# A finished head's accumulator is copied out of its bank by DVE ahead of two exps, in place of ACT between them

## The chip, the cores and the metric

The kernel runs on one core of one Trainium2 chip. The metric is the device time of one execution in microseconds. Before the change three runs took 3089.30, 3089.61 and 3089.72 us: a median of 3089.61 us. One further execution was profiled. It took 3089.38 us, of which 3087.6 us lie between its first and its last instruction (the span).

Names of engines: PE or TensorE (matmuls; PEld are its weight loads), DVE or VectorE, ACT or ScalarE, POOL or GpSimd, SP (issues DMAs). Each works through its own instructions strictly in the order in which the program has issued them.

## The reference

One layer of an encoder over 4096 tokens with 16 meta tokens ahead of them. What matters here is the attention branch: 8 query heads over 2 key/value heads, each of dimension 64, softmax over all 4112 keys, no mask.

```python
def gqa_block(q_blk, k, v):
    s = jnp.einsum('bkgqd,bksd->bkgqs', q_blk, k).astype(jnp.float32) * (HEAD_DIM ** -0.5)
    p = jax.nn.softmax(s, axis=-1)
    return jnp.einsum('bkgqs,bksd->bkgqd', p.astype(v.dtype), v)
...
a_out = attention_branch(q, k, v, q_norm_g[i], k_norm_g[i], cos, sin, n_tok) * jax.nn.silu(a_gate)
mixed = jnp.concatenate([f_out, a_out], axis=-1)
h = h + jnp.einsum('ble,ed->bld', mixed, w_out[i])
```

Beside it runs a Fourier branch (a DFT over positions and channels), then an output projection with residual, and a final RMSNorm.

## The kernel before

`phase_a` makes the projections (until some 770 us), `phase_b` the DFT, the attention and the output. All of what follows is in `phase_b`. The order of the work on each engine is the order of the calls in the program (`tc.manual_schedule()`); the framework adds only the semaphores that the data need.

**Tiling.** Queries go in 8 blocks b of 512. For each block there are 4 pairs p of heads, so the main loop (L1449) runs over 32 pairs i. A pair has two heads, one after the other, and each head 33 units: one for each chunk of 128 keys, in the order `SEQ` (the meta chunk first, then 0, 1, 4, 5, 2, 3, 6, 7, 8, 9, 12, ...). Unit j of a pair has number n = j % 33 within its head. `step` makes the four parts of a unit:

- `qk` (L1195): scores of 128 keys x 512 queries in a PSUM bank `s`. There are two such banks (`pq`). A chunk with n % 8 < 4 starts a bank anew (two matmuls, L1202 and L1203). The chunk four further on is kept as a difference of keys and is added on top of that bank (one matmul, L1198, and a half matmul in `low`, L1207), after the first chunk's exp has read it. So each score matmul waits for the exp of an earlier unit.
- `low` (L1205): the half matmuls of two difference chunks, run together.
- `ex` (L1209): ACT computes exp into `pe` (L1212); then DVE or POOL subtracts the upper 16 bits, giving the rest `rr` in 16 bits (L1214).
- `pvm` (L1217): nine matmuls (L1229 to L1236) that add the unit's probabilities times V, in high and low parts, to the head's accumulator `o`, a bank of the pool `pv` with one buffer. The next head's first `pvm` must therefore wait until the last head's `o` has been read. For the last unit, `pvm` returns `end`.

**The end of a head.** `end` (L1240) copies 452 columns of `o` to `tt` (L1243, ACT), takes the reciprocal of the sums (L1245, DVE), and four POOL instructions (L1247 to L1250) add the parts, multiply by the gate and by the reciprocal, and put the result in `ob`.

**Order of a unit.** In the loop over j: `qk()`, then a matmul of the output projection of the block before (`plan`, L1309; in units with n % 4 != 0). At the units with n = 4, 8, ..., 32 (`RUNS`) the `low` of two units follows; then `draw()` issues four matmuls of the row-maximum work of the next pair (`grp` in `max_units`, L1119); then `ex` of the two units; then one of two `parts` of the row-maximum work (a relu on ACT, L1124, and a max pass on DVE, L1125). The other units with n % 4 != 3 have their `ex` and one part. At the end of each unit its `pvm` is put in `pend`, and the one of five units before is issued (`LAG` = 5). At n = 4 the last `pvm` of the old head is drawn ahead of `low` (L1478), and its `end` is issued between the two `ex` (L1486). At the very end of the loop the last head's `end` comes from `flush`.

**Who subtracts.** `on_dve` (L1458): units with n = 0 and with n % 4 of 2 or 3 on DVE, the others on POOL; in the last pair DVE has every j not divisible by 3.

**The first five pairs** (`block0`) run the DFT's matmuls and the work behind them between the units, in place of the output projection. The last pair has no row-maximum work. After the loop a tail does the output projection of the last block.

In the text "the first run" of a head is the stretch from its units 3 and 4's `low` (n = 4) to the next `low` (n = 8); "the second run" is from n = 8 to n = 12.

Of the kernel before, what the change touches and what calls it, by code (L numbers as in the profile page):

```python
# [26 lines left out]
AF = mybir.ActivationFunctionType  # L27
# [768 lines left out]
def phase_b(tc, a, pool, mm3, id32, id16, sc):  # L796
# [5 lines left out]
    V, S, T, G = nc.vector, nc.scalar, nc.tensor, nc.gpsimd  # L802
# [4 lines left out]
    with ExitStack() as st:  # L807
# [383 lines left out]
        def step(h, kv, t, n, qa, qb, acc, banks, ob, gate, last):  # L1191
            d = {}
            cs = slice(n * P, (n + 1) * P)

            def qk():  # L1195
                if n < NT and n % 8 >= 4:
                    s = d["s"] = banks.pop(n - 4)
                    T.matmul(s, K[kv][:, 0, cs], qa, start=False, stop=False, skip_group_check=True)  # L1198
                else:
                    late = kv and last and n < NT and n // 2 % 2  # L1200
                    s = d["s"] = banks[n] = (pm if late else pq).tile([P, 512], F32, tag="m" if late else "s", name="s")
                    T.matmul(s, K[kv][:, 0, cs], qa, start=True, stop=False)  # L1202
                    T.matmul(s, K[kv][:, 1, cs], qb, start=False, stop=True)  # L1203

            def low(x):  # L1205
                r = slice(64 * x, 64 * x + 64)
                T.matmul(d["s"], K[kv][r, 1, cs], (qb if x else qa)[r], start=False, stop=True, skip_group_check=True)  # L1207

            def ex(eng):  # L1209
                pe = wk.tile([P, 512], F32, tag="pe", name="pe")  # L1210
                rr = wk.tile([P, 512], F16, tag="rr", name="rr")
                S.activation(pe, d["s"], AF.Exp, scale=HD ** -0.5)  # L1212
                hi = pe.bitcast(BF16)[:, 1::2]
                eng.tensor_tensor(out=rr, in0=pe, in1=hi, op=ALU.subtract)  # L1214
                d["hi"], d["rr"] = hi, rr

            def pvm():  # L1217


                if t == 0:  # L1220
                    acc.append(pv.tile([P, 512], F32, tag="o", name="o"))
                o = acc[0]
                hi, rr = d["hi"], d["rr"]
                vh, va, vl = VV[:, n, kv, :65], VV[:, n, kv], VV[:, n, kv, 65:129]
                for s in range(4):
                    cs = slice(s * P, (s + 1) * P)
                    c0 = s * 129
                    if s < 3:
                        T.matmul(o[:, c0:c0 + 129], hi[:, cs], va, start=t == 0 and s == 0, stop=t == NT,  # L1229
                                 skip_group_check=True)  # L1230
                    else:
                        T.matmul(o[:, c0:c0 + 65], hi[:, cs], vh, start=False, stop=t == NT,  # L1232
                                 skip_group_check=True)
                        T.matmul(o[:, c0:c0 + 64], hi[:, cs], vl, start=False, stop=t == NT,  # L1234
                                 skip_group_check=True)
                    T.matmul(o[:, c0:c0 + 65], rr[:, cs], vh, start=False, stop=t == NT, skip_group_check=True)  # L1236
                if t < NT:
                    return

                def end():  # L1240
                    tt = w2.tile([P, 452], F32, tag="tt", name="tt")
                    rc = sm.tile([P, 4], F32, tag="rc", name="rc")
                    S.activation(tt, o[:, :452], AF.Copy)  # L1243
                    tv = tt[:, :387].rearrange("p (s c)->p s c", s=3)
                    V.reciprocal(out=rc, in_=tt[:, 64:452:129])  # L1245
                    dst = ob[:, :, h * HD:(h + 1) * HD]
                    G.tensor_tensor(out=dst[:, 0:3], in0=tv[:, :, 0:64], in1=tv[:, :, 65:129], op=ALU.add)  # L1247
                    G.tensor_tensor(out=dst[:, 0:3], in0=dst[:, 0:3], in1=gate[:, 0:3], op=ALU.mult)
                    G.tensor_tensor(out=dst[:, 3], in0=tt[:, 387:451], in1=gate[:, 3], op=ALU.mult)
                    G.tensor_tensor(out=dst, in0=dst, in1=rc.unsqueeze(2).broadcast_to([P, 4, HD]), op=ALU.mult)  # L1250

                return end

            return qk, low, ex, pvm
# [187 lines left out]
        def flush():  # L1442

            end = pend.pop(0)()
            if end:
                end()

        prev = None
        for i, (b, p) in enumerate(pairs):  # L1449
            if p == 1 and b + 1 < NQB:  # L1450
                qload(b + 1)
            if i > 4:
                load_xr(b - 1, p)
            elif i == 4:
                load_mf(0, 0)
            ready = {}
            halves = out_units(b - 1, p) if b > 0 else None
            on_dve = {j for j in range(66) if j % 33 == 0 or j % 33 % 4 in (2, 3)}  # L1458
            if i + 1 == len(pairs):
                on_dve = {j for j in range(2 * NT + 2) if j % 3}  # L1460
            units = stream(i)
            plan = {}
            if halves:
                plan = dict(zip(OUT if i > 4 else OUT0, halves[0][0] + halves[0][1]))
            for j, (qk, half, ex, pvm) in enumerate(units):
                n = j % 33
                if n == 5:
                    for z in (j, j + 1):
                        if z in plan:
                            plan.pop(z)()  # L1470
                qk()
                if j == 63 and i + 1 < len(pairs):
                    fin_()
                    put_()
                if j in plan:
                    plan[j]()
                if j in RUNS:
                    end = pend.pop(0)() if n == 4 and pend else None  # L1478
                    units[j - 1][1](0)
                    half(1)  # L1480
                    more = draw()
                    if more:
                        parts.extend(more())
                    for x in (j - 1, j):
                        units[x][2](V if x in on_dve else G)
                        if end:  # L1486
                            end()
                            end = None
                    if parts:
                        parts.pop(0)()  # L1490
                elif n % 4 != 3:
                    ex(V if j in on_dve else G)
                    if parts:
                        parts.pop(0)()
                if j == (TR if i > 4 else 12) and b > 0:
                    low = out_tr(b - 1, p)
                last = {}
                if i + 1 < len(pairs):
                    meta_, red_, fin_, put_ = ends.get(i + 1, (None,) * 4)
                    last = {60: red_}  # L1500
                    if j == MT and meta_:
                        meta_[0]()
                if j in last:
                    last[j]()
                if i < 5:
                    block0(66 * i + j, j - 2 in RUNS)
                if i == 4 and j == 28:
                    load_xr(0, 0)
                if i == 4 and j == 6:
                    ready = dict(zip((7, 8, 9), mf_parts(0, 0)))  # L1510
                if i + 1 == len(pairs):
                    if 20 <= j < 60 and j % 11 == 9:
                        load_mf(b, j // 11 - 1)
                    if j >= 26 and j % 11 == 4:
                        ready = dict(zip((j, j + 1, j + 2), mf_parts(b, j // 11 - 2)))
                elif i >= 4:
                    if j == 40:
                        load_mf(*divmod(i - 3, 4))
                    if j == 47:
                        ready = dict(zip((48, 52, 53), mf_parts(*divmod(i - 3, 4))))  # L1520
                if j in ready:
                    ready[j]()
                if j == LAG + 2 and i + 1 < len(pairs):
                    gload(i + 1)
                if j == 20 and i + 1 == len(pairs):
                    load_xr(b, 0)
                if j == (TR if i > 4 else 12) + 1 and b > 0:
                    low()
                if j in NORM and prev:
                    prev[NORM.index(j)]()  # L1530
                if j == 65 and b > 0:
                    prev = out_end(b - 1, p, halves[1])
                pend.append(pvm)
                if len(pend) > LAG:
                    flush()
# [222 lines left out]
```

## Time and profile before

| | |
|---|---|
| median of three runs | 3089.61 us |
| the profiled execution | 3089.38 us, span 3087.6 us |
| granted TensorE clock, mean | 0.997 |
| PE / PEld busy | 3033.3 / 1798.9 us |
| DVE / ACT / POOL busy | 2248.5 / 2013.2 / 1737.6 us |
| L1243, the copy on ACT | 64 times, 542 ns each, 34.7 us |
| L1212, exp on ACT | 2112 times, 611 ns each |
| L1125, max pass on DVE | 1024 times, 689 ns each |

A row of the timeline reads: start in us from the span's start, duration in us, engine, line, operation, output <- inputs, shapes, number of like instructions merged in the row, and in brackets how long the engine had been idle before it and what ended that. Ends of matmuls are modelled, their starts are not. A row of a line's own view has the count, the shortest, median and longest duration in ns, and the first and the last start in us.

### The profile page before, as it was taken

How to read it: one execution, taken by the hardware profiler on the slowest of the kernel's cores; microseconds unless marked ns; L12 is line 12 of the kernel's file. 1: busy time of each engine (PE TensorE's matmuls, PEld its weight loads, DVE VectorE, ACT ScalarE, POOL GpSimd, SP SyncE). 2: the span in 40 equal slices, each digit the busy share in tenths (PEclk: the TensorE clock that was granted, in tenths of full speed). 3: DMA queues.
4: the chain of work that ended last, by engine and by line, in shares of the span. 5: the costliest groups of instructions: out<-in, count | busy, mean ns of one | idle time of the engine just before them, and what ended most of it. 6: DMA issues, size and time to landing. Idle time of an engine off the chain costs nothing.

```text
span 3087.6 us, 80210 instructions
## 1 busy us (share of the span) xinstructions
PE 3033.3 (98%) x32000; PEld 1798.9 (58%) x32000; DVE 2248.5 (73%) x4865; ACT 2013.2 (65%) x3936; POOL 1737.6 (56%) x1642
## 2 busy tenths in 40 slices
PE   8999999998999999999999999999999999999998
PEld 4555555555666655555555555555555555555564
DVE  6656565656878777777777777777777777777775
ACT  6434333325777777777777777777777777777763
POOL 4655555644767655555555555555555555555552
PEclk9999999999999999999999999999999999999999
DMA  7545445555521221112112111211121121111112
GB/s 243 183 149 172 133 139 169 166 179 181 135 74 43 79 55 29 33 35 49 29 32 43 43 33 32 50 29 39 29 50 29 39 46 33 32 32 29 39 41 71
DMA packets 236765, 235.23 MB, mean 76 GB/s; under 512 B 136949, under 2 KB 180949, under 8 KB 233573
## 3 DMA queue, kind: packets, MB, share of 16 engines
q1 hardware_dynamic: 222564, 204.93, 23.6%
q10 hardware_dynamic: 13824, 25.17, 2.2%
q8 instruction: 250, 4.10, 0.5%
q14 instruction: 127, 1.03, 0.1%
HBM read 131.14 MB, written 66.38 MB: 64 GB/s over the span
## 4 chain that ended last, share of the span: by engine, by line
PE 70%; ACT 2%; DVE 1%; POOL 1%; issue 1%; ACTq 0%; POOLq 0%; DVEq 0%
PE o L1229 12%; PE po L1309 10%; PE o L1236 8%; PE s L1198 7%; PE s L1202 7%; PE s L1203 7%; PE m L1119 6%; PE s L1207 5%; PE o L1234 2%; PE o L1232 2%; PE m L1557 1%; ACT pe L1212 1%; POOL rr L1214 1%; PE pd L913 1%; DVE rl L1125 0%
## 5 line engine op out<-in xcount | busy, mean ns | idle before, releaser
L1212 ACT ACTIVATE pe<-s 128x512 f32<-128x512 f32 x2112 | 1242.4, 611 | 571.9 <-PE s L1207 516.7
L1214 POOL TENSOR_TENSOR rr<-pe 128x512 f16<-128x512 f32 x1014 | 1131.3, 1133 | 797.4 <-ACT pe L1212 797.2
L1214 DVE TENSOR_TENSOR rr<-pe 128x512 f16<-128x512 f32 x1098 | 890.0, 812 | 275.3 <-ACT pe L1212 272.2
L1236 PE MATMUL o<-VV,rr 128*128 128x65 f16 x8448 | 974.7, 193 | 1.9 <-POOL rr L1214 1.8
L1236 PEld LDWEIGHTS <-rr 128*128 128x128 f16 x8448 | 784.2, 98 | 186.2 <-POOL rr L1214 3.1
L1125 DVE CUSTOM_DVE_ANT_0 rl<-m,rl 128x512 f32<-128x512 f32 x1024 | 703.7, 689 | 249.6 <-ACT rl L1124 248.7
L1229 PE MATMUL o<-VV,pe 128*128 128x129 f16 x6336 | 839.8, 221 | 0.4 <-ACT tt L1243 0.4
L1229 PEld LDWEIGHTS <-pe 128*128 128x128 bf16 x6336 | 590.6, 97 | 357.3 <-issue 183.0
L1124 ACT ACTIVATE rl<-m 128x512 f32<-128x512 f32 x1024 | 631.9, 619 | 8.6 <-PE m L1119 6.1
L1202 PE MATMUL s<-qA,K 128*128 128x512 f16 x1088 | 410.8, 378 | 3.6 <-ACT pe L1212 3.0
L1203 PE MATMUL s<-qB,K 128*128 128x512 f16 x1088 | 411.3, 378 | 0.0
L1232 PE MATMUL o<-VV,pe 128*128 128x65 f16 x2112 | 411.3, 195 | 0.0
L1234 PE MATMUL o<-VV,pe 128*128 128x64 f16 x2112 | 410.5, 194 | 0.0
L1198 PE MATMUL s<-qA,K 128*128 128x512 f16 x1024 | 387.2, 378 | 8.2 <-ACT pe L1212 4.0
L330 PE MATMUL ps<-wh,xh 128*128 128x512 f16 (+2 forms) x1032 | 352.0, 353 | 8.7 <-ACT xh L318 8.7
L331 PE MATMUL ps<-wl,xh 128*128 128x512 f16 (+2 forms) x1032 | 352.0, 353 | 2.6 <-DVE wl L301 2.4
L1119 PE MATMUL m<-K,qA 64*128 64x512 f16 x1024 | 305.4, 377 | 10.2 <-ACT rl L1124 4.7
L1119 PE MATMUL m<-K,qB 64*128 64x512 f16 x1024 | 306.8, 377 | 1.2 <-DVE mx L1125 0.7
L333 PE MATMUL ps<-wh,xl 128*128 128x512 f16 x768 | 291.1, 379 | 0.0
L1234 PEld LDWEIGHTS <-pe 128*128 128x128 bf16 x2112 | 209.1, 99 | 0.0
L1232 PEld LDWEIGHTS <-pe 128*128 128x128 bf16 x2112 | 206.4, 98 | 0.0
L1207 PE MATMUL s<-qB,K 64*128 64x512 f16 x512 | 197.9, 386 | 0.0
(218 smaller groups left out, 4358.6 us busy)
## 6 DMA issues: line engine op xcount, KB each, us to landing
room<-x SPq DMA_DIRECT2D x32, 512.0 KB
xt<-xt SPq DMA_DIRECT2D x32, 512.0 KB
sg<-fx SPq DMA_DIRECT2D x16, 1024.0 KB
xr<-x SPq DMA_DIRECT2D x32, 512.0 KB
out<-yo SPq DMA_DIRECT2D x32, 512.0 KB
fg_d<-g ACTq DMA_DIRECT2D x32, 256.0 KB
ag_d<-g ACTq DMA_DIRECT2D x32, 256.0 KB
q_d<-qs ACTq DMA_DIRECT2D x32, 256.0 KB
```

What stands on the lines that cost most here:

```text
L1119: T.matmul(ts[x], q[e][p][:, e, s * P:(s + 1) * P], K[kv][64 * e:64 * e + 64, 0, c0:c0 + 512], start=True, stop=True)
L1124: S.activation(rl, ts[e], AF.Relu)
L1125: V.tensor_tensor_reduce(out=rl, in0=ts[2 + e], in1=rl, scale=1.0, scalar=-3.0e38, op0=ALU.add, op1=ALU.max, accum_out=mx[:, s, e, o:o + 1])
L1198: T.matmul(s, K[kv][:, 0, cs], qa, start=False, stop=False, skip_group_check=True)
L1202: T.matmul(s, K[kv][:, 0, cs], qa, start=True, stop=False)
L1203: T.matmul(s, K[kv][:, 1, cs], qb, start=False, stop=True)
L1212: S.activation(pe, d["s"], AF.Exp, scale=HD ** -0.5)
L1214: eng.tensor_tensor(out=rr, in0=pe, in1=hi, op=ALU.subtract)
L1229: T.matmul(o[:, c0:c0 + 129], hi[:, cs], va, start=t == 0 and s == 0, stop=t == NT, skip_group_check=True)
L1232: T.matmul(o[:, c0:c0 + 65], hi[:, cs], vh, start=False, stop=t == NT, skip_group_check=True)
L1234: T.matmul(o[:, c0:c0 + 64], hi[:, cs], vl, start=False, stop=t == NT, skip_group_check=True)
L1236: T.matmul(o[:, c0:c0 + 65], rr[:, cs], vh, start=False, stop=t == NT, skip_group_check=True)
```

## The change

The copy of the accumulator is done by DVE (`tensor_copy`) and no longer by ACT. And in the units of `RUNS`, `end` is issued ahead of both `ex`, no longer between them.

```diff
@@ end() in step()
                     tt = w2.tile([P, 452], F32, tag="tt", name="tt")
                     rc = sm.tile([P, 4], F32, tag="rc", name="rc")
-                    S.activation(tt, o[:, :452], AF.Copy)
+                    V.tensor_copy(tt, o[:, :452])
                     tv = tt[:, :387].rearrange("p (s c)->p s c", s=3)
                     V.reciprocal(out=rc, in_=tt[:, 64:452:129])
@@ the loop over units, j in RUNS
                     more = draw()
                     if more:
                         parts.extend(more())
+                    if end:
+                        end()
                     for x in (j - 1, j):
                         units[x][2](V if x in on_dve else G)
-                        if end:
-                            end()
-                            end = None
                     if parts:
                         parts.pop(0)()
```

## The prediction

> **What bounds the kernel now.** I read the page first. TensorE is busy nearly all the time and no other engine is near it.
>
> ```profile
> span 3087.6 us, 80210 instructions
> PE 3033.3 (98%) x32000; PEld 1798.9 (58%) x32000; DVE 2248.5 (73%) x4865; ACT 2013.2 (65%) x3936; POOL 1737.6 (56%) x1642
> ```
>
> By this the change, which only shifts 0.54 us of work per head from ACT to DVE, should do nothing: neither engine is full. The view of the copy's own line seems to agree. Its second line here stands under "who waited for it": TensorE waited for the copy twice, 0.4 us in all.
>
> ```profile
> L1243 ACT ACTIVATE tt<-o x64: 539/542/547, 813.3 to 3035.2; 128x452 f32<-128x452 f32 x64
> ...
>   PE o L1229: 0.4, 2
> ```
>
> But the ends of matmuls are modelled, so a wait shorter than a matmul's modelled length shows as busy. Starts are real, so next I compared starts. Here are TensorE's rows around the first run of the head that begins near 2023 us (a run is the stretch from one L1207 to the next, four units of keys).
>
> ```profile
> 2023.25 0.19 PE L1236 MATMUL o<-VV,rr 128*128 128x65 f16 x1
> 2023.37 0.39 PE L1207 MATMUL s<-qA,K 64*128 64x512 f16 x1
> ...
> 2025.00 0.22 PE L1229 MATMUL o<-VV,pe 128*128 128x129 f16 x1
> ...
> 2025.43 0.38 PE L1202 MATMUL s<-qA,K 128*128 128x512 f16 x1
> ...
> 2026.41 0.38 PE L1198 MATMUL s<-qA,K 128*128 128x512 f16 x1
> ...
> 2027.39 0.38 PE L1198 MATMUL s<-qA,K 128*128 128x512 f16 x1
> 2027.70 0.39 PE L1207 MATMUL s<-qA,K 64*128 64x512 f16 x1
> ...
> 2027.92 0.38 PE L1119 MATMUL m<-K,qA 64*128 64x512 f16 x1
> ...
> 2031.26 0.22 PE L1229 MATMUL o<-VV,pe 128*128 128x129 f16 x1
> ...
> 2031.61 0.38 PE L1198 MATMUL s<-qA,K 128*128 128x512 f16 x1
> 2031.92 0.39 PE L1207 MATMUL s<-qA,K 64*128 64x512 f16 x1
> ```
>
> The second run lasts 2031.92 - 2027.70 = 4.22 us. The first lasts 4.33 us, though it holds one set of PV matmuls fewer: the set of the old head's last unit was drawn ahead of it (it ends with the row at 2023.25), so three sets lie in it, not four. One set costs 2031.61 - 2031.26 = 0.35 us. The first run's work is thus 4.22 - 0.35 = 3.87 us, and 4.33 - 3.87 = 0.46 us of it is waiting, though the profile calls it busy. ACT's rows say for what.
>
> ```profile
> 2023.85 0.60 ACT L1212 ACTIVATE pe<-s 128x512 f32<-128x512 f32 x1 [1.64 <-PE s L1207]
> 2024.35 0.54 ACT L1243 ACTIVATE tt<-o 128x452 f32<-128x452 f32 x1
> 2024.77 0.60 ACT L1212 ACTIVATE pe<-s 128x512 f32<-128x512 f32 x1
> 2025.25 0.62 ACT L1124 ACTIVATE rl<-m 128x512 f32<-128x512 f32 x1
> 2025.73 0.63 ACT L1212 ACTIVATE pe<-s 128x512 f32<-128x512 f32 x1
> ...
> 2026.68 0.66 ACT L1212 ACTIVATE pe<-s 128x512 f32<-128x512 f32 x1
> ...
> 2028.18 1.09 ACT L1212 ACTIVATE pe<-s 128x512 f32<-128x512 f32 x2 [0.84 <-POOL rr L1214]
> 2029.15 0.60 ACT L1124 ACTIVATE rl<-m 128x512 f32<-128x512 f32 x1
> ```
>
> There are two score banks, so a unit's score matmul waits for the exp of the unit two before it. The exps end at 2024.77 + 0.60 = 2025.37, 2026.36 and 2027.34, and TensorE's score matmuls start 0.05 to 0.07 us behind each: 2025.43, 2026.41, 2027.39. From 2023.85 to 2027.34 ACT has no gap. For this one run per head ACT sets the end, and the copy at 2024.35 stands in its chain. In the second run the two exps follow each other directly and TensorE has a fourth PV set to cover them, so nothing waits.
>
> This is no accident of one head. The first and last head of the 52 between (pairs 5 to 30) have the same run:
>
> ```profile
> 1143.44 0.39 PE L1207 MATMUL s<-qA,K 64*128 64x512 f16 x1
> ...
> 1147.77 0.39 PE L1207 MATMUL s<-qA,K 64*128 64x512 f16 x1
> ...
> 2938.76 0.39 PE L1207 MATMUL s<-qA,K 64*128 64x512 f16 x1
> ...
> 2943.09 0.39 PE L1207 MATMUL s<-qA,K 64*128 64x512 f16 x1
> ```
>
> Both last 4.33 us. [...]
>
> **The change part by part.** *The copy leaves ACT.* From first exp to first relu is 2025.25 - 2023.85 = 1.40 us with the copy between, and 2029.15 - 2028.18 = 0.97 us without it (the two exps of the row at 2028.18). So all that follows on ACT comes 0.43 us sooner: the exp that ended at 2027.34 ends at 2026.91, and releases TensorE at 2026.96. TensorE's own work would bring it to that matmul at 2023.37 + 3.87 - (2027.70 - 2027.39) = 2026.93. The two meet: the next run starts near 2027.27 in place of 2027.70. I take 0.43 us a head; it can't be more than the 0.46 us of waiting. For 52 heads: 22.4 us.
>
> *The copy comes to DVE.* DVE's rows of the same time, with one more that I need below, and POOL's:
>
> ```profile
> 2022.24 0.96 DVE L1214 TENSOR_TENSOR rr<-pe 128x512 f16<-128x512 f32 x1 [0.23 <-ACT pe L1212]
> 2024.48 0.69 DVE L1214 TENSOR_TENSOR rr<-pe 128x512 f16<-128x512 f32 x1 [1.28 <-ACT pe L1212]
> ...
> 2026.88 0.69 DVE L1125 CUSTOM_DVE_ANT_0 rl<-m,rl 128x512 f32<-128x512 f32 x1 [0.28 <-ACT rl L1124]
> ...
> 2031.38 1.24 DVE L1214 TENSOR_TENSOR rr<-pe 128x512 f16<-128x512 f32 x1
> ```
>
> ```profile
> 2024.97 0.59 POOL L1247 TENSOR_TENSOR ob<-tt 128x192 f32<-128x192 f32 x1 [2.31 <-ACT tt L1243]
> ...
> 2027.14 4.93 POOL L1214 TENSOR_TENSOR rr<-pe 128x512 f16<-128x512 f32 x4
> ```
>
> No row has DVE copying 452 columns out of a bank. Its cost lies between ACT's 0.54 us and the 0.69 us that DVE takes for 512 columns from a bank at L1125; I take 0.65, since it is the same engine with a tenth fewer columns. [...]
>
> DVE is free from 2022.24 + 0.96 = 2023.20. The bank is complete at 2023.25 + 0.19 = 2023.44; with the 0.09 us that ACT needs after TensorE (2023.37 + 0.39 to 2023.85) the copy runs from 2023.53 to about 2024.2, and the reciprocal follows it. The next subtraction isn't due before 2024.48, its exp being what it waits for (1.28 us idle). So the copy lies in idle time of DVE and costs nothing on the path; without that cover it would shift DVE by its 0.65 us. What waits for it: TensorE's first write into the bank, at 2025.00, some 0.8 us later; and POOL's four operations, which start about 0.7 us sooner. Queued behind the copy on DVE are that subtraction, the two max passes and the next subtraction. No DMA and nothing of SP is moved. On POOL the order stays: unit 3's subtraction is DVE's, unit 4's stood behind the four operations already.
>
> *Other heads.* The last pair has no max work and splits the subtractions otherwise:
>
> ```profile
> 2973.89 0.39 PE L1207 MATMUL s<-qA,K 64*128 64x512 f16 x1
> ...
> 2977.70 0.39 PE L1207 MATMUL s<-qA,K 64*128 64x512 f16 x1
> ...
> 2981.50 0.39 PE L1207 MATMUL s<-qA,K 64*128 64x512 f16 x1
> ```
>
> Its first run waits 3.81 - (3.80 - 0.35) = 0.36 us. But there unit 3's subtraction is POOL's and is now issued behind the four operations (2027.14 - 2024.97 = 2.17 us) instead of ahead; its PV set is the first of the next run, and I reckon that the delay takes the gain back: 0 for both heads. The nine heads of pairs 0 to 4 share the engines with the DFT. Eight could save 0.43 us each, 3.4 in all; in one DVE is late:
>
> ```profile
> 999.12 0.22 PE L1229 MATMUL o<-VV,pe 128*128 128x129 f16 x1
> ...
> 999.28 0.55 DVE L959 COPY thl<-thl 128x512 f16<-128x512 f16 x1
> 999.75 0.68 DVE L1214 TENSOR_TENSOR rr<-pe 128x512 f16<-128x512 f32 x1
> ```
>
> The copy would take the subtraction's place at 999.75 and end near 1000.4, where TensorE wanted the bank at 999.12: up to 1.3 us lost. Bounds -1.3 to +3.9 (nine times 0.43); I take 2, since most of these heads look like the later ones but what they win may end in another wait. The last head's copy, in the tail, is behind 48 output matmuls: 0.
>
> *Sum:* 22.4 + 2 + 0 = 24.4 us. The profiled execution took 3089.38 us (span 3087.6 and 1.8 around it), so 3065.0; the median, 3089.61, lies 0.2 us above it, so 3065.2.
>
> **The rivals.** *DVE's subtraction is caught by POOL* (the slower side). POOL's four operations now start near 2024.25, ahead of the subtraction at 2024.48; before, they started at 2024.97, behind its start. While POOL works, a DVE subtraction can stretch: 1.24 us at 2031.38, inside POOL's 4.93 us, and the line's spread is wide.
>
> ```profile
> L1214 DVE TENSOR_TENSOR rr<-pe x1098: 669/692/2661, 774.0 to 3034.0; 128x512 f16<-128x512 f32 x183
> ```
>
> Behind it stand the two max passes, the second of which (now to start near 2026.88 - 0.43 = 2026.45) must be done when TensorE's next max matmul wants its bank, at 2027.92 - 0.43 = 2027.49. Two passes of some 0.7 us before 2027.49 mean that the subtraction has to end by about 2026.1, so it may last 1.6 us from 2024.48. At 1.85 us half the gain is lost (about 3077); from 1.6 + 0.43 = 2.05 us the change loses; at 2.66 us, the longest here, it loses 1.05 - 0.43 = 0.6 us a head, 32 us in 52 heads: 3121. Against it: POOL's pieces are 0.3 to 0.6 us long there, and 1.24 us, the typical stretched one, is under the bound. [...]
>
> *Nothing gained.* TensorE at 98% is the bound and the starts mislead, or the exps after the copy are held by something else: 3089.4. For it: 0.4 us of waits put down to the copy. Against it: three score matmuls standing 0.05 to 0.07 us behind three exps, in every head.
>
> *Half gained.* The first step of the rival above, or TensorE finding another wait within the run: about 3077.
>
> *The copy doesn't move as said.* Where the last unit's PV set isn't drawn early there is no copy ahead of the exps; that is only the tail's, one of 64.
>
> **How the numbers follow.** Forecast (3060 to 3070): 0.76. Half gained: 0.10. Nothing: 0.08. Slower: 0.06. The low end is 3089.6 less 52 x 0.46 and 3.9, with rounding 3061; I put 3060. The high end takes in half a gain: 3077. That leaves out a little under 2 in 10. A change of under 0.2%, 6 us, can't be told from none here; so faster 0.86, same 0.08, slower 0.06.
>
> **What would show it.** In the changed profile the first run of a head should last about 3.9 us in place of 4.33, with two exps directly behind each other and the relu 0.97 us after the first; a copy row on DVE of 0.6 to 0.7 us in the former gap; TensorE's first PV matmul not waiting on it; the second run still 4.2 us. I am wrong if first runs stay above 4.1 us, if DVE's first subtraction lasts over 1.6 us, or if the second run grows by what the first lost.

## The result, and the profile after

The changed kernel takes 3063.86 us (median of four runs, 3063.00 to 3066.74), the kernel before 3089.66 us beside it: a ratio of 0.9921, 95% interval 0.9910 to 0.9933. The prediction was 3065.2 us. The profiled execution took 3063.76 us.

The page after, its first lines:

```profile
span 3062.0 us, 80210 instructions
PE 3008.4 (98%) x32000; PEld 1789.8 (58%) x32000; DVE 2290.6 (75%) x4929; ACT 1985.5 (65%) x3872; POOL 1750.1 (57%) x1642
```

TensorE's share of busy time is 98% as before. But its busy time has fallen by 3033.3 - 3008.4 = 24.9 us with the same 32000 matmuls: what went was waiting that was booked as work.

The copy's own line after (durations in ns as shortest/median/longest; then what its engine waited for, and who waited for it):

```profile
L1243 DVE COPY tt<-o x64: 614/629/629, 811.2 to 3009.6; 128x452 f32<-128x452 f32 x64
its engine sat idle before it (us, times) until:
  PE o L1236: 17.9, 58
...
  PE o L1229: 0.9, 1
```

In 58 of 64 heads DVE was idle and waited for the bank; in one TensorE waited for the copy. Now the same head that the prediction showed (it begins at 2008.67 here). TensorE:

```profile
2008.67 0.39 PE L1207 MATMUL s<-qA,K 64*128 64x512 f16 x1
...
2010.30 0.22 PE L1229 MATMUL o<-VV,pe 128*128 128x129 f16 x1
...
2010.65 0.38 PE L1202 MATMUL s<-qA,K 128*128 128x512 f16 x1
...
2011.44 0.38 PE L1198 MATMUL s<-qA,K 128*128 128x512 f16 x1
...
2012.25 0.38 PE L1198 MATMUL s<-qA,K 128*128 128x512 f16 x1
2012.56 0.39 PE L1207 MATMUL s<-qA,K 64*128 64x512 f16 x1
...
2016.79 0.39 PE L1207 MATMUL s<-qA,K 64*128 64x512 f16 x1
```

The first run lasts 3.89 us (4.33 before), the second 4.23 (4.22 before). ACT, DVE and POOL in the same stretch:

```profile
2009.15 1.09 ACT L1212 ACTIVATE pe<-s 128x512 f32<-128x512 f32 x2 [1.64 <-PE s L1207]
2010.13 0.60 ACT L1124 ACTIVATE rl<-m 128x512 f32<-128x512 f32 x1
2010.60 0.62 ACT L1212 ACTIVATE pe<-s 128x512 f32<-128x512 f32 x1
...
2011.56 0.64 ACT L1212 ACTIVATE pe<-s 128x512 f32<-128x512 f32 x1
```

```profile
2008.78 0.63 DVE L1243 COPY tt<-o 128x452 f32<-128x452 f32 x1 [0.27 <-PE o L1236]
...
2009.79 0.78 DVE L1214 TENSOR_TENSOR rr<-pe 128x512 f16<-128x512 f32 x1 [0.17 <-ACT pe L1212]
```

```profile
2009.49 0.53 POOL L1247 TENSOR_TENSOR ob<-tt 128x192 f32<-128x192 f32 x1 [1.53 <-DVE tt L1243]
2010.10 0.92 POOL L1248 TENSOR_TENSOR ob<-ob,ag 128x192 f32<-128x192 f32 x1
...
2011.92 4.93 POOL L1214 TENSOR_TENSOR rr<-pe 128x512 f16<-128x512 f32 x4
```

The relu comes 0.98 us after the first exp in place of 1.40. The exp that ended 3.97 us into the run (2027.34 - 2023.37) ends 3.53 us into it (2011.56 + 0.64 - 2008.67). Before, all three score matmuls shown in the prediction stood 0.05 to 0.07 us behind the end of an exp. Now the first two start 0.41 and 0.22 us behind theirs (2010.24 and 2011.22), so ACT no longer holds them; only the last, at 2012.25, still stands 0.05 us behind its exp (2012.20). The copy fills the gap that DVE had, and the subtraction behind it still waits for its exp.

**By stage.** The first half matmuls (L1207) of heads 0, 1, 10 (pair 5) and 62 (the last pair) cut the span into stages. Heads are counted from 0, and the copy of a head's bank stands in the next head's first run; so head 0 holds no copy. After:

```profile
773.15 0.39 PE L1207 MATMUL s<-qA,K 64*128 64x512 f16 x1
...
810.97 0.39 PE L1207 MATMUL s<-qA,K 64*128 64x512 f16 x1
...
1139.56 0.39 PE L1207 MATMUL s<-qA,K 64*128 64x512 f16 x1
1143.45 0.39 PE L1207 MATMUL s<-qA,K 64*128 64x512 f16 x1
...
2946.92 0.39 PE L1207 MATMUL s<-qA,K 64*128 64x512 f16 x1
```

The same starts before were 775.97, 812.35, 1143.44 and 2973.89.

| stage | before | after | difference | forecast |
|---|---|---|---|---|
| up to the first head's first run | 775.97 | 773.15 | -2.8 | - |
| head 0, without a copy | 36.4 | 37.8 | +1.4 | - |
| heads 1 to 9 (to the end of pair 4) | 331.1 | 328.6 | -2.5 | -2 |
| pairs 5 to 30 | 1830.5 | 1807.4 | -23.1 | -22.4 |
| last pair and tail | 113.7 | 115.1 | +1.4 | 0 |
| span | 3087.6 | 3062.0 | -25.6 | -24.4 |

In the first two stages the two kernels run the same instructions. The first differs from execution to execution (768.1 to 776.0 us over the profiles below). Head 0 took 36.4 us in three of the profiles below (before and the last two of the table), 39.4 in one (ACT ahead of the exps) and 37.8 in the other six, among them the one that differs from the kernel before only in the engine that copies. In the changed kernel one subtraction on DVE lasts 4.73 us there, beside POOL's; the like one before is the 2.66 us that the prediction names as the longest.

```profile
785.59 4.73 DVE L1214 TENSOR_TENSOR rr<-pe 128x512 f16<-128x512 f32 x1
```

Totals of one kernel scatter by several us (the kernel before took 3083.43 to 3090.79 us in one set of 14 runs), while the stage of pairs 5 to 30 took 1807.4 us in both profiles of the changed kernel. So the experiments are read by that stage first.

### The profile page after: what moved, and what is told of

Read it like the earlier page. It is cut to its first block, busy times and chain, and to the rows that moved or that the text cites. A ratio compares the mean times of both kernels' runs of the same rounds, so it can differ in the third digit from the quotient of the medians.

```text
span 3062.0 us, 80210 instructions
## 1 busy us (share of the span) xinstructions
PE 3008.4 (98%) x32000; PEld 1789.8 (58%) x32000; DVE 2290.6 (75%) x4929; ACT 1985.5 (65%) x3872; POOL 1750.1 (57%) x1642
## 4 chain that ended last, share of the span: by engine, by line
PE 90%; POOL 2%; DVE 2%; ACT 2%; issue 2%; DMA 1%; SPq 0%; ACTq 0%; POOLq 0%; DVEq 0%
PE o L1229 12%; PE po L1309 10%; PE o L1236 8%; PE s L1202 7%; PE s L1203 7%; PE s L1198 7%; PE m L1119 7%; PE ps L330 6%; PE ps L331 6%; PE ps L333 5%; PE s L1207 5%; PE o L1234 2%; PE o L1232 2%; PE m L1556 1%; ACT pe L1212 1%
## 5 line engine op out<-in xcount | busy, mean ns | idle before, releaser
L1207 PE MATMUL s<-qB,K 64*128 64x512 f16 x512 | 197.8, 386 | 0.0
```

## The experiments

The starts of head 10 and of head 62 in each profile, and the first two runs of head 35, in the middle:

| kernel | head 10 | head 62 | pairs 5 to 30 | head 35, first run | second run |
|---|---|---|---|---|---|
| before | 1143.44 | 2973.89 | 1830.5 | 4.33 | 4.22 |
| after | 1139.56 | 2946.92 | 1807.4 | 3.89 | 4.23 |
| after, once more | 1140.29 | 2947.68 | 1807.4 | 3.89 | 4.23 |
| DVE, between the exps | 1142.60 | 2992.06 | 1849.5 | 4.63 | 4.29 |
| ACT, ahead of the exps | 1137.13 | 2948.04 | 1810.9 | 3.95 | 4.23 |
| after, with another copy on ACT | 1144.74 | 2975.48 | 1830.7 | 4.33 | 4.23 |
| after, DVE's copy made twice | 1136.71 | 2954.36 | 1817.7 | 3.89 | 4.42 |
| after, a second copy beside POOL | 1140.40 | 2948.11 | 1807.7 | 3.89 | 4.23 |
| POOL's operations between the exps | 1138.54 | 2945.89 | 1807.4 | 3.89 | 4.22 |
| and one copy on ACT | 1138.86 | 2946.44 | 1807.6 | 3.89 | 4.22 |

Three theories stood against each other. Chain: the copy's slot between two exps on ACT was what TensorE waited for. Load: ACT is relieved of 64 copies. Bank: TensorE gets the accumulator's bank back sooner.

### The engine alone: DVE's copy at the old place

```diff
 def end():   (issued between the two ex, as before)
-    S.activation(tt, o[:, :452], AF.Copy)
+    V.tensor_copy(tt, o[:, :452])
```

> The copy goes to DVE, but stays at its old place between the two exps. Theory of the chain (the gain is that the two exps follow each other on ACT, and DVE's copy is free only ahead of its first subtraction): ACT is free of the copy, but on DVE the copy now stands behind a subtraction that waits for the first exp, starts near 1.75 us into the first run and ends near 2.4 us, and TensorE wants the bank at 1.63 us; the first run of a head lasts about 4.67 us in place of 4.33, some 18 us more in 52 heads: 3105 to 3112 us. Rival of the load (any copy taken from ACT helps, wherever it is issued): about 3064 us.

Measured: 3112.54 us, ratio 1.0079 (1.0064 to 1.0094): slower. ACT has no copy here, and it doesn't help. DVE's rows in head 35 (from 2031.94), and TensorE's first write to the bank:

```profile
2033.05 0.69 DVE L1214 TENSOR_TENSOR rr<-pe 128x512 f16<-128x512 f32 x1 [1.28 <-ACT pe L1212]
2033.66 0.62 DVE L1243 COPY tt<-o 128x452 f32<-128x452 f32 x1
```

```profile
2034.34 0.22 PE L1229 MATMUL o<-VV,pe 128*128 128x129 f16 x1 [0.60 <-DVE tt L1243]
```

The copy stands behind a subtraction that itself waits 1.28 us for an exp, so the bank comes free at 2.34 us into the run, 0.7 us after TensorE wants it. The waits of TensorE (us in total, times, longest) have it in first place:

```profile
PE o L1229 <- DVE tt L1243: 38.5, 61, 1.6
```

First runs grew as expected (4.63 us in head 35), and pairs 5 to 30 take 19.0 us more than before; the total lies 0.5 us above the range expected, and pairs 0 to 4 take 5.8 us more, which the expectation left out. That DVE's free slot is only ahead of the subtraction is shown. The load theory said about 3064 us and misses; but here the late bank could hide a gain, so it takes the next experiment to refute it.

### The order alone: ACT's copy ahead of the exps

```diff
 def end():   (issued ahead of both ex, as in the changed kernel)
-    V.tensor_copy(tt, o[:, :452])
+    S.activation(tt, o[:, :452], AF.Copy)
```

> The copy stays on ACT, but is issued ahead of both exps. Theory of the chain: ACT sits idle before the first exp of the run (1.64 us), the bank is complete 0.4 us before that exp can start, so the copy runs from about 0.11 to 0.65 us into the run and pushes the exps back by only some 0.08 us; first run 3.95 to 4.0 us, so about 18 of the 22 us: 3069 to 3073 us. Rival of the load (it is DVE in place of ACT that helps): 3089 us. Rival of the bank (it is TensorE getting the bank sooner that helps): 3064 us, since the bank is read by 0.65 us here.

Measured: 3066.32 us, ratio 0.9932 (0.9915 to 0.9948); pairs 5 to 30 take 1810.9 us, 19.5 less than before and 3.5 more than with DVE. ACT, in head 35 (from 2007.60):

```profile
2007.70 0.55 ACT L1243 ACTIVATE tt<-o 128x452 f32<-128x452 f32 x1 [1.26 <-PE o L1236]
2008.15 1.08 ACT L1212 ACTIVATE pe<-s 128x512 f32<-128x512 f32 x2
```

ACT too had idle time ahead of the exps. There the copy delays the first exp by 0.07 us (0.55 in place of 0.48 us into the run). So of the 23.1 us of that stage 19.5 come with the order alone, and the engine adds 3.5 once the order is right; without it the engine costs 19.0. ACT makes all 64 copies here and the gain comes all the same, so the load theory falls. The total lies below the expected 3069 to 3073 us; in this profile the stage ahead of the attention was short (769.43 us), which the change doesn't touch.

### An unrelated copy put back on ACT

```diff
 for x in (j - 1, j):
     units[x][2](V if x in on_dve else G)
+    if end:
+        S.activation(dum, VV[:, 0:2].rearrange("p t a c->p (t a c)")[:, 0:432], AF.Copy)
+        end = None
```

> The changed kernel, with a copy added on ACT between the two exps that has nothing to do with the bank: 432 16-bit columns from SBUF to an unused tile. Theory of the chain: the exps behind it are late again by some 0.45 us, the first run lasts 4.3 to 4.4 us again: 3085 to 3092 us. Rival of the bank: the bank is free as early as in the changed kernel, so 3064 us.

Measured: 3091.16 us, ratio 1.0008 (0.9999 to 1.0017): the whole gain is gone, with the bank freed as early as in the changed kernel. DVE's copy starts 0.11 us into the run in both (2024.93 - 2024.82 here, 2008.78 - 2008.67 there).

```profile
2024.93 0.63 DVE L1243 COPY tt<-o 128x452 f32<-128x452 f32 x1 [0.27 <-PE o L1236]
```

```profile
2025.30 0.60 ACT L1212 ACTIVATE pe<-s 128x512 f32<-128x512 f32 x1 [1.64 <-PE s L1207]
2025.80 0.56 ACT L1490 ACTIVATE dum<-VV 128x432 f16<-128x432 f16 x1
2026.25 0.59 ACT L1212 ACTIVATE pe<-s 128x512 f32<-128x512 f32 x1
2026.73 0.60 ACT L1124 ACTIVATE rl<-m 128x512 f32<-128x512 f32 x1
```

Relu follows the first exp by 1.43 us, and the first run is 4.33 us again. The bank theory falls: an early bank alone brings nothing (a late one costs, as with DVE's copy at the old place). Of the three theories only the chain is left, and it foretold all three results in kind: what TensorE waits for is the time between those exps, 0.45 us here, whatever the instruction there does.

### DVE's copy made twice

```diff
     V.tensor_copy(tt, o[:, :452])
+    V.tensor_copy(tt, o[:, :452])
```

> The changed kernel, with DVE's copy made twice, the second over the first. Theory (the copy lies in idle time of DVE, with some 0.9 us before TensorE wants the bank): the second copy ends near 1.35 us into the run, TensorE wants the bank at 1.63 us, the first subtraction is late by about 0.35 us and nothing waits for it; first run still 3.89 us: 3063 to 3067 us. Rival (DVE's time does count, so that the gain is what ACT loses less what DVE gets): 64 more copies at 0.63 us each take up to 40 us; with half of it, 3084 us.

Measured: 3077.48 us, ratio 0.9964 (0.9951 to 0.9977). I had missed. The first run is 3.89 us as expected, but the second grew to 4.42 us. POOL's four operations wait for the second copy and start 0.65 us later in the run (2012.29 - 2010.82 in place of 2009.49 - 2008.67); POOL's subtractions come behind them. Two rows of POOL, and TensorE's PV set of unit 5 in the second run (from 2014.71):

```profile
2012.29 0.53 POOL L1248 TENSOR_TENSOR ob<-tt 128x192 f32<-128x192 f32 x1 [2.19 <-DVE tt L1244]
...
2014.73 5.38 POOL L1214 TENSOR_TENSOR rr<-pe 128x512 f16<-128x512 f32 x4
```

```profile
2017.48 0.22 PE L1229 MATMUL o<-VV,pe 128*128 128x129 f16 x1
2017.72 0.20 PE L1236 MATMUL o<-VV,rr 128*128 128x65 f16 x1
```

The second matmul of the set, which needs the rest `rr`, starts 0.24 us after the first in place of 0.06. POOL's second subtraction in that row, unit 5's, ends at 2016.18 + 1.48 = 2017.66, just ahead of the matmul at 2017.72:

```profile
2016.18 1.48 POOL L1214 TENSOR_TENSOR rr<-pe 128x512 f16<-128x512 f32 x1
```

I took that for the cause; but DVE is late in the first run as well. By its second max pass it is on time again (2013.90 - 2010.82 = 3.08 us into the run, 2011.74 - 2008.67 = 3.07 in the changed kernel).

### The same extra time on DVE, beside POOL's path

```diff
     V.reciprocal(out=rc, in_=tt[:, 64:452:129])
+    V.tensor_copy(dum, o[:, :432])
```

> The changed kernel with a second copy out of the bank on DVE, of 432 columns to an unused tile, behind the reciprocal; so DVE has the same extra time as with the copy made twice, but POOL's four operations don't wait for it. Theory of POOL (with the copy made twice the second run grew from 4.23 to 4.41 us because POOL began later and its second subtraction came late): second runs are back at 4.23 to 4.25 us, total 3062 to 3067 us. Rival of DVE (the second run grew because DVE's own subtractions and max passes were late): second runs stay near 4.4 us, total about 3073 us.

Measured: 3067.71 us, ratio 0.9938 (0.9923 to 0.9953). Pairs 5 to 30 are back at 1807.7 us and the second run at 4.23. DVE's added copy (it is named CAST, 0.58 us) follows the reciprocal; POOL doesn't wait for it:

```profile
2010.50 0.53 POOL L1250 TENSOR_TENSOR ob<-tt 128x192 f32<-128x192 f32 x1 [1.53 <-DVE tt L1245]
...
2013.08 2.49 POOL L1216 TENSOR_TENSOR rr<-pe 128x512 f16<-128x512 f32 x2
```

The row at 2013.08 has two of POOL's subtractions. They begin 3.40 us into the run; with the copy made twice the first began at 3.91 (2014.73 - 2010.82), in the changed kernel at 3.25 (2011.92 - 2008.67). So DVE has another 0.6 us of room in that stage, and POOL has less than 0.65: the growth of the second run was POOL's lateness. DVE was not quite as late here as with the copy made twice (its first subtraction ends 2.04 us into the run, there 2.55), so it is the two findings together, this one and DVE's catching up there, that clear DVE. The total is 0.7 us above the range expected; the five first pairs take 1.6 us more than in the changed kernel (their first run begins at 772.43, head 10 at 1140.40), so among them DVE's extra time does count.

### POOL's operations put back between the exps

```diff
-    if end:
-        end()
+    rest = end() if end else None    # copy and reciprocal on DVE
     for x in (j - 1, j):
         units[x][2](V if x in on_dve else G)
+        if rest:
+            rest()                   # the four operations of POOL
+            rest = None
```

This undoes one part of the change, in the last pair alone. The changed kernel ran once more beside it.

> The changed kernel once more, to hold the next two against it on the same chip. Where the first unit's half matmul of the attention comes has differed by up to 8 us between executions so far (768 to 776 us), with nothing changed ahead of it: first runs 3.90 us in the 52 heads of pairs 5 to 30, the last pair 59.8 us from its first to its last run, total 3060 to 3066 us.

> DVE's copy and reciprocal stay ahead of both exps, POOL's four operations go back between them. Only the last pair sees another order on POOL (there the first of the two subtractions is POOL's). Theory (the last pair loses because that subtraction stands behind the four operations): its second runs go from 4.76 and 4.99 us back to 3.80 to 4.1 us, the last pair's stretch from 59.8 to about 57.7 us; pairs 5 to 30 as in the changed kernel; about 2 us less in all. Rival (the last pair loses because DVE has the copy): its second runs stay at 4.8 to 5.0 us and the time is that of the changed kernel.

Measured: the changed kernel again 3063.63 us, ratio 0.9921 (0.9909 to 0.9934); with POOL's operations between 3061.55 us, 0.9918 (0.9904 to 0.9931). The changed kernel came as expected: the last pair takes 59.8 us from its first to its last run, and pairs 5 to 30 again 1807.4. The totals can't be told apart; the rows can. First the changed kernel, then this one, at the first head of the last pair, TensorE:

```profile
2946.92 0.39 PE L1207 MATMUL s<-qA,K 64*128 64x512 f16 x1
...
2950.37 0.39 PE L1207 MATMUL s<-qA,K 64*128 64x512 f16 x1
...
2951.71 0.20 PE L1236 MATMUL o<-VV,rr 128*128 128x65 f16 x1 [0.79 <-POOL rr L1214]
...
2955.13 0.39 PE L1207 MATMUL s<-qA,K 64*128 64x512 f16 x1
```

```profile
2949.33 0.39 PE L1207 MATMUL s<-qA,K 64*128 64x512 f16 x1
...
2953.13 0.39 PE L1207 MATMUL s<-qA,K 64*128 64x512 f16 x1
```

The second run goes from 4.76 to 3.80 us, with the gain of the first kept. For this head the theory holds: POOL's subtraction of unit 3 had been put behind the four operations. In the second head the second run goes from 4.99 to 4.34 us only, above the 3.80 to 4.1 expected, and TensorE still waits for POOL there:

```profile
2984.45 0.20 PE L1236 MATMUL o<-VV,rr 128*128 128x65 f16 x1 [0.37 <-POOL rr L1214]
```

The last pair's stretch is 58.2 us, where 57.7 was expected. Pairs 0 to 4 took 1.4 us less than in the changed kernel, all of it in head 0, which holds no copy; so of the 2.7 us between the two spans (3062.0 and 3059.3) only 1.6, in the last pair, are due to this edit.

### And one copy left to ACT

```diff
-    rest = end() if end else None
+    rest = end((i, j) == (3, 4)) if end else None    # true: ACT copies
```

> As the kernel with POOL's operations between the exps, and in the one head of the first five pairs whose copy stands behind the DFT's work on DVE (pair 3, first head) the copy is left to ACT, ahead of both exps. Theory (that head lost 0.9 us because TensorE waits for DVE's late copy): its first run goes from 5.31 us to about 4.2 us, and TensorE no longer waits for a copy on DVE; about 1 us less than with POOL's operations between alone, 3 us less than the changed kernel, which is near what five rounds can tell.

Measured: 3061.82 us, ratio 0.9917 (0.9904 to 0.9931). In the changed kernel TensorE waits in that head for the late copy:

```profile
994.24 0.39 PE L1207 MATMUL s<-qA,K 64*128 64x512 f16 x1
...
996.84 0.22 PE L1229 MATMUL o<-VV,pe 128*128 128x129 f16 x1 [0.88 <-DVE tt L1243]
...
999.55 0.39 PE L1207 MATMUL s<-qA,K 64*128 64x512 f16 x1
```

Its first run, 5.31 us, is 4.32 us with the copy on ACT (994.37 to 998.69). The 1 us is visible there (pairs 0 to 4 take 364.1 us, 365.0 without this edit) and not in the total. Both of these last kernels lie 2 us under the changed one, which is within their intervals.

## Why the prediction was right

*The hidden wait.* Right. It was read from starts, 0.46 us a first run, and 0.44 of it is gone; 52 heads gave 23.1 us where 22.4 were forecast, 22.4 of it in the first runs themselves. The unrelated copy on ACT brought all of it back, and the early copy on ACT kept 19.5 of it, which together show the cause. The matmul busy share showed none of it: it was 98% before and 98% after, since waiting was booked as work (3033.3 us busy before, 3008.4 after, for the same 32000 matmuls).

*The copy's price and its cover.* Right: 0.63 us measured, 0.65 taken, in DVE's idle time, with TensorE's first write 0.9 us behind its end (2008.78 + 0.63 to 2010.30). The cover is DVE's slot ahead of the subtraction: one place later this stage takes 19.0 us more than before the change, and 42 more than with the copy in the slot.

*The last pair.* Wrong by 1.4 us. The step "I reckon that the delay takes the gain back: 0 for both heads" failed in size. The subtraction of unit 3 was late as said, but the 2.17 us for POOL's four operations had been read in another head. In the last pair's first head they took 2.92 us before the change too (2978.35 + 0.61 - 2976.04):

```profile
2976.04 0.98 POOL L1247 TENSOR_TENSOR ob<-tt 128x192 f32<-128x192 f32 x1
...
2978.35 0.61 POOL L1250 TENSOR_TENSOR ob<-ob,rc 128x256 f32<-128x256 f32 x1
```

After it the wait is 0.79 us as shown, and the second run is 0.96 us longer, against a gain of 0.36 in the first. In the second head it is 1.19 against 0.44.

*The first five pairs.* Right: 2 us taken, 2.5 measured in the nine heads that hold a copy. (With head 0, which holds none, the two profiles differ by 1.1 only.) The one head whose copy would be late behind DVE's DFT work was named; it lost 0.92 us (4.39 to 5.31), where up to 1.3 was the bound.

*The slower rival.* Its first step came, its price didn't: the subtraction caught by POOL's operations lasts 0.78 us in place of 0.69, where 1.6 was the point from which it would decide. The 4.73 us above are past any of its prices, but stand in head 0, ahead of the first copy. What stood nearer was not in the prediction: POOL's second subtraction, which the copy made twice brought into the path. In pairs 5 to 30 the queue of POOL behind `end`, not that of DVE, has the least room.

*The total.* Of the 25.6 us between the two profiles 2.8 lie ahead of the attention, and head 0 takes 1.4 back. Both stand ahead of the first copy, and both vary among kernels that are alike there, so I count neither. What is left is 2.5 + 23.1 - 1.4 = 24.2 us, where 24.4 were forecast. That closeness is luck in part: the stages miss by 0.5, 0.7 and 1.4 us, and the first two offset the third. That the first stage's 2.8 us is chance is not shown, since the kernel before was profiled once; the medians of two sets of runs put the whole gain at 25.8 us (3089.66 - 3063.86) and 24.1 us (3087.73 - 3063.63).

## What to carry to other kernels

Where matmul ends are modelled, compare the starts of like stretches of work and count what each holds: a stretch that has less work and takes longer hides a wait, however busy its engine looks (here 4.33 us against 4.22, with one PV set of 0.35 us fewer, on an engine booked as busy for 98% of the span). An instruction between two links of a chain cost time here even on an engine that was idle a third of the time (0.43 us of the copy's 0.54, with ACT 65% busy), and next to nothing a place earlier, where that engine waited anyway (0.07 us on ACT, in a wait of 1.64 us); the order was worth 19.5 us here and the engine 3.5 on top of it, while the engine without the order cost 19.0. After such a move, follow what is queued behind the moved work on every engine that it feeds, since the next limit was on the third one (POOL, 0.65 us late with the copy made twice, took the second run from 4.23 to 4.42 us).

## What the runs showed that I had not expected

The stage ahead of the attention differs by up to 8 us between executions of kernels that are alike there (768.1 to 776.0 us), and the stage of pairs 5 to 30 by 0.2 us at most among the two profiles of the changed kernel and the last two of the table, which do the same work in it (1807.4 to 1807.6). Why the first stage varies stays open, and so does what decides between 36.4 and 37.8 us in head 0.

ACT's instructions overlap in the rows: in the kernel before the copy starts at 2024.35, while the exp ahead of it lasts until 2023.85 + 0.60 = 2024.45. The 452-column copy lasts 542 ns, but taking it out moved the exps by 0.43 us only. DVE's copy of the same columns takes 629 ns.

DVE's and POOL's operations took longer in some rows in which they ran beside each other. L1248 on POOL took 0.92 us beside DVE's subtraction (the row at 2010.10), and 0.59 us before the change, when no DVE subtraction ran beside it; over its 64 times the median went from 595 to 922 ns. That subtraction of DVE's took 0.78 us in place of 0.69. POOL's four subtractions, with DVE's beside them in both, took 5.38 us with the copy made twice and 4.93 in the changed kernel. No run here varied this alone, so the cause is not shown.
